# Gates and output projection of a hybrid decoder block as block products of seven multiplications

## The chip, the cores and the metric

The kernel runs on one core of a Trainium2 chip. The metric is the device time of one execution in microseconds (us), and of several runs the median. One execution is also recorded by the profiler, and the rows below come from that one. The engines are named as in the profile: PE is TensorE (matmul), PEld its weight load, DVE is VectorE, ACT is ScalarE, POOL is GpSimd, SP is SyncE. In this kernel SP issues the loads and POOL issues the stores, each as a queue in a fixed order.

## What is computed

One pre-norm decoder block on a sequence of 2048 tokens and 1024 channels (D), in float32, and a last RMS norm. Cut to what matters here:

```python
u = _rmsnorm(h, norm_mix_g[l])
z = jnp.einsum('bsd,dn->bsn', u, w_in[l])
q, k, v, pz, ga, gp = jnp.split(z, offs, axis=-1)
a = _attention_branch(q, k, v).astype(dt)               # (S, 256)
p = _pool_branch(pz, w_pool_grp[l], pool_scale[l]).astype(dt)   # (S, 768)
merged = (jax.nn.sigmoid(ga) * jnp.einsum('bsc,cd->bsd', a, w_att_out[l])
          + jax.nn.sigmoid(gp) * jnp.einsum('bsc,cd->bsd', p, w_pool_out[l]))
h = h + jnp.einsum('bsd,de->bse', merged, w_out[l])
m = _rmsnorm(h, norm_mlp_g[l])
hid = jnp.square(jax.nn.relu(jnp.einsum('bsd,df->bsf', m, w_mlp_in[l])))   # (S, 4096)
h = h + jnp.einsum('bsf,fd->bsd', hid, w_mlp_out[l])
return _rmsnorm(h, norm_final_g)
```

The gates `ga` and `gp` and the output projection `w_out` are products with 1024 x 1024 matrices; the two inner products of `merged` have 256 and 768 input channels.

## The kernel before

Activations lie transposed: 128 channels on the partitions, 512 tokens (a chunk, C) along the row, so a piece is a tile of 128 x 512 and 256 KB. Every operand of a matmul is split in two float32r parts, a rounded high part (a cast on ACT) and the rest (a subtraction on DVE), and each product is made of three matmuls, high x high, high x low and low x high (`mm3` L119, `mm_acc` L612). Such a split costs one ACT and one DVE instruction for each weight and each activation tile.

The stages follow each other on PE: a fold of the pooling weights, then projections and attention (a1, a2, a3, up to L497), then stage b (L506 to L589), the first MLP product c1 (L647 to L744), and the second with the last norm, c2 (L747 to L877). `schedule_with_timeline_sim=True` lets a scheduler put the instructions of each engine in order; each engine then works its list strictly in that order.

At the end of attention (L474 to L497), DVE makes the weights of the three head groups (`nm`), POOL stores them to DRAM (`wts_d`), SP loads them back broadcast over partitions as six tiles `wb` (three buffers), and DVE multiplies and adds these into `af`, which POOL stores to `a_d`.

Stage b goes chunk by chunk, four times: the normed input `u` is computed again from `x` (`norm_x`, L166); for each of 8 output blocks `gate` (L513) loads, splits and multiplies a gate weight; the pooling and the attention product follow, `mf` and `mt` are the gated values, and their sum is split into `mh`, `ml`. Then come 8 blocks of the output projection: the residual `h` is loaded by SP (L575), DVE adds the product from PSUM to it, POOL stores `h` (`h_d`) and the gained `hg` (`hg_d`), ACT squares it and DVE adds the squares up in `hss`, which is stored once per chunk. All products here are plain: 8 x 3 matmuls of 128 x 512 for an output block with 1024 input channels.

Stages c1 and c2 use block products of seven multiplications instead of eight. Weights are taken as 2 x 2 blocks A11 to A22 and activations as 2 x 2 blocks B11 to B22 (halves of the input channels, and the two chunks of one half of the sequence). Sums of weights S1 to S4 and of activations T1 to T4 are made on DVE (`sums` L674), seven products are accumulated in PSUM, and three intermediate results are copied out by ACT (`zS`, `zA`) and added to later products by DVE. In c1 the order of the seven is `ORDER1` (L688), two weight pairs j work side by side, and activations are combined and split once for each half, at its first pairs. PSUM has eight banks. In c2 each half begins with the factor of the MLP norm (`z_st`, a matmul of `hss` with ones, L133, loaded at L798) and the last norm of a chunk (`z_fst`, from `fss`) stands right after its last product (L874, L877).

## Time and profile before

| what | value |
|---|---|
| median of 3 runs | 2897.25 us (2895.51 to 2898.23) |
| the profiled execution | 2892.27 us, its span 2890.5 us |
| mean granted clock of PE | 0.966 |
| PE busy | 2700.0 us, 93%, 13254 matmuls |
| DVE, ACT, POOL busy | 1723.3, 1302.5, 281.9 us |
| DMA | 356.14 MB on the hardware queue (SP), 94.49 MB on the software queue (POOL) |
| first matmul of stage b, first `z_st` of c2 | 829.24, 2193.4 us |

Busy time is summed by engine and says nothing of which stage waits; starts in a row are microseconds from the span's beginning, and `[x <- ...]` behind an instruction is the engine's idle time before it and what ended it.

### The profile page before, as it was taken

To read this page: it belongs to the slowest core of one execution; us is meant where nothing else is said; L and a number is where in the kernel's file an instruction comes from. 1 tells how busy PE (TensorE), PEld (TensorE's weight loads), DVE (VectorE), ACT (ScalarE), POOL (GpSimd) and SP (SyncE) were. 2 spreads that over 40 slices of the span, in tenths; PEclk is the share of its full clock that TensorE was granted. 3 is DMA by queue.
4 is the path that set the end of the run, shared out by engine and by line. 5 is a ranking of instruction groups with operands and counts; after the bars stand their busy time and mean duration, and the time that the engine had idled before them with its cause. 6 is when DMAs were issued, how large, how long until landed. Compare 5 with 4: busy or idle time off the path is not lost.

```text
span 2890.5 us, 36706 instructions
## 1 busy us (share of the span) xinstructions
PE 2700.0 (93%) x13254; PEld 2222.9 (77%) x13254; DVE 1723.3 (60%) x2588; ACT 1302.5 (45%) x2304; POOL 281.9 (10%) x429
## 2 busy tenths in 40 slices
PE   8999999789787999999998999989998999879996
PEld 7887788668676888888886788878886788768885
DVE  5469847455555635446246666766665665757557
ACT  5434444334343424334234555655554444544444
POOL 3034200000000000101000222112221000000000
PEclk9999999899898999999999999999999999989998
DMA  7234443323215544635336555545558556753433
GB/s 259 82 109 165 150 156 112 101 89 111 94 63 182 167 144 134 208 128 187 116 100 207 199 190 189 193 168 181 184 190 312 171 166 196 237 159 108 130 106 128
DMA packets 185030, 452.98 MB, mean 157 GB/s; under 512 B 23216, under 2 KB 30384, under 8 KB 184720
## 3 DMA queue, kind: packets, MB, share of 16 engines
q1 hardware_dynamic: 156096, 356.14, 38.5%
q0 software_dynamic: 28752, 94.49, 8.6%
q8 instruction: 104, 1.70, 0.3%
q14 instruction: 78, 0.64, 0.1%
HBM read 347.68 MB, written 102.86 MB: 156 GB/s over the span
## 4 chain that ended last, share of the span: by engine, by line
PE 46%; issue 41%; DMA 5%; DVE 5%; POOL 2%; ACT 1%; SPq 0%; POOLq 0%; DVEq 0%; ACTq 0%
PE z L616 7%; PE z L617 6%; PE z L615 6%; PE z_b L617 3%; PE z_b L616 3%; PE z_b L615 3%; PE z_c L616 2%; PE z_c L615 2%; PE z_c L617 2%; PE mm_v L270 2%; DMA r<-in_w 1%; PE mm L122 1%; PE mm L124 1%; PE mm L123 1%; DMA x<-hid_d 1%
## 5 line engine op out<-in xcount | busy, mean ns | idle before, releaser
L124 PE MATMUL mmb_bg<-xh_b,lo_bg 128*128 128x512 f32 x512 | 200.1, 391 | 11.6 <-DVE lo_bg L116 11.6
L122 PE MATMUL mmb_bg<-xh_b,hi_bg 128*128 128x512 f32 x512 | 200.0, 391 | 0.0
L123 PE MATMUL mmb_bg<-xl_b,hi_bg 128*128 128x512 f32 x512 | 199.9, 390 | 0.0
L116 DVE TENSOR_TENSOR lo_bg<-raw_bg,hi_bg 128x1024 fp32r<-128x1024 f32 x64 | 78.2, 1222 | 143.2 <-ACT hi_bg L115 143.0
L609 DVE TENSOR_TENSOR wl_S<-r_S,wh_S 128x512 fp32r<-128x512 f32 x128 | 88.4, 690 | 123.7 <-ACT wh_S L608 123.7
L608 ACT CAST wh_S<-r_S 128x512 fp32r<-128x512 f32 x128 | 79.8, 624 | 175.5 <-PE z L616 157.4
L616 PE MATMUL z<-xl_T,wh_S 128*128 128x512 f32 x384 | 149.6, 390 | 2.8 <-DVE xl_T L609 2.8
L617 PE MATMUL z<-xh_T,wl_S 128*128 128x512 f32 x384 | 149.4, 389 | 0.0
L609 DVE TENSOR_TENSOR wl_S<-s,wh_S 128x512 fp32r<-128x512 f32 x128 | 86.6, 689 | 99.8 <-ACT wh_S L608 99.8
L115 ACT CAST hi_bg<-raw_bg 128x1024 fp32r<-128x1024 f32 x64 | 67.4, 1053 | 171.1 <-PE mmb_bg L123 144.3
L615 PE MATMUL z<-xh_T,wh_S 128*128 128x512 f32 x384 | 138.7, 389 | 0.0
L311 ACT ACTIVATE sb_g<-sb_g,negm 128x256 f32<-128x256 f32 (+1 forms) x192 | 86.3, 451 | 96.6 <-DVE negm L309 96.5
L124 PEld LDWEIGHTS mmb_bg<-xh_b,lo_bg 128*128 128x128 f32 x512 | 96.6, 189 | 32.1 <-DVE lo_bg L116 12.0
L609 DVE TENSOR_TENSOR wl_A<-r_A,wh_A 128x512 fp32r<-128x512 f32 x96 | 66.0, 689 | 88.8 <-ACT wh_A L608 88.5
L608 ACT CAST wh_S<-s 128x512 fp32r<-128x512 f32 x128 | 77.2, 618 | 88.6 <-PE z_c L616 43.6
L608 ACT CAST wh_A<-r_A 128x512 fp32r<-128x512 f32 x96 | 59.5, 622 | 123.5 <-PE z L616 88.3
L122 PEld LDWEIGHTS mmb_bg<-xh_b,hi_bg 128*128 128x128 f32 x512 | 96.5, 189 | 20.2
L123 PEld LDWEIGHTS mmb_bg<-xl_b,hi_bg 128*128 128x128 f32 x512 | 96.5, 189 | 20.1
L615 PE MATMUL z<-xh_B,wh_A 128*128 128x512 f32 x256 | 99.4, 404 | 4.6 <-ACT xh_B L608 4.6
L124 PE MATMUL mm_a<-xh_a,lo_a 128*128 128x512 f32 x256 | 102.2, 400 | 0.0
L123 PE MATMUL mm_a<-xl_a,hi_a 128*128 128x512 f32 x256 | 101.7, 398 | 0.0
L616 PE MATMUL z<-xl_B,wh_A 128*128 128x512 f32 x256 | 101.3, 396 | 0.0
(330 smaller groups left out, 8008.5 us busy)
## 6 DMA issues: line engine op xcount, KB each, us to landing
r<-in_w SPq DMA_DIRECT2D x96, 512.0 KB
x<-hid_d SPq DMA_DIRECT2D x160, 256.0 KB
raw_bg<-in_w_gates SPq DMA_DIRECT2D x64, 512.0 KB
r_S<-w2s_d SPq DMA_DIRECT2D x128, 256.0 KB
x_a<-in_xt SPq DMA_DIRECT2D x96, 256.0 KB
r_A<-in_w SPq DMA_DIRECT2D x96, 256.0 KB
raw_a<-in_w_qk SPq DMA_DIRECT2D x32, 512.0 KB
raw_bw<-in_w_o SPq DMA_DIRECT2D x32, 512.0 KB
```

The lines of the kernel that those rows point to most:

```text
L115: nc.scalar.copy(hi, raw)
L116: (lo_on or nc.vector).tensor_sub(lo, raw, hi.bitcast(F32))
L122: nc.tensor.matmul(ps, lh, rh, start=(i == 0), stop=False)
L123: nc.tensor.matmul(ps, lh, rl, start=False, stop=False)
L124: nc.tensor.matmul(ps, ll, rh, start=False, stop=(i == n - 1))
L270: nc.tensor.matmul(pv[t][:, :256], a, b, start=(k == 0 and n == 0), stop=(k == KD - 1 and n == 2))
L311: nc.scalar.activation(s[:, h, :W], s[:, h, :W], AF.Exp, bias=negm[:, col + h:col + h + 1], accum_out=l[:, col + h:col + h + 1])
L608: nc.scalar.copy(hi, src)
L609: nc.vector.tensor_sub(lo, src, hi.bitcast(F32))
L615: nc.tensor.matmul(ps, lh, rh, start=start and i == 0, stop=False, skip_group_check=True)
L616: nc.tensor.matmul(ps, lh, rl, start=False, stop=False, skip_group_check=True)
L617: nc.tensor.matmul(ps, ll, rh, start=False, stop=stop and i == n - 1, skip_group_check=True)
```

## The change

Stage b is taken out. `norm_x`, as attention calls it, now also stores `u` to DRAM (`u_d`), with three buffers instead of two. One pool `wp` serves four kinds of stages, each run for half of the sequence (1024 tokens): `gates` (the 16 gate blocks as block products of `u_d`, sigmoid on ACT, stored to `sg_d`), `merge` (the pooling and attention products as before, with the gates loaded back, stored to `mg_d`), `residual` (the output projection as block products of `mg_d`) and `mlp_in` (c1 as before). In `residual` the block leaves PSUM as the intermediate tiles do; a DMA of POOL with `accum_op` adds `xt` into the tile, another stores it to `h_d`, ACT squares it, a third DMA adds the squares up in DRAM (`hss_d`), ACT multiplies by the gain in place, and a fourth stores to `hg_d`. The order of the stages is written at the end: gates of half 0, merge 0, gates 1, residual 0, merge 1, mlp_in 0, residual 1, mlp_in 1. In c2 the factor is made at the second of the seven products, and the last norms are put off to the seventh weight pair of the product that comes next.

```diff
+    u_d = dram.tile([KD, P, SEQ], F32, name="u_d")
+    sg_d = dram.tile([2 * KD, P, SEQ], F32, name="sg_d")
+    mg_d = dram.tile([KD, P, SEQ], F32, name="mg_d")
...
-        u = io.tile([P, C], F32, name=f"u_{key}", tag="xu", bufs=2)
+        u = io.tile([P, C], F32, name=f"u_{key}", tag="xu", bufs=3)
...
-            normed(load_x(c, k, key), g_mix[:, k:k + 1], rstd[:, c * C:(c + 1) * C], hi, lo, f"{key}_{k}")
+            u = normed(load_x(c, k, key), g_mix[:, k:k + 1], rstd[:, c * C:(c + 1) * C], hi, lo, f"{key}_{k}")
+            nc.gpsimd.dma_start(u_d[k, :, c * C:(c + 1) * C], u)
...
-    with ExitStack() as st:
-        bp = pool_of(st, "b")
...
-            ssq = bp.tile([P, C], F32, name=f"hss_{c}", tag="hss", bufs=1)
-            for e in range(KD):
-                w = split_load(w_o[e], D, f"bw_{c}_{e}")
-                h = bp.tile([P, C], F32, name=f"h_{c}_{e}", tag="h", bufs=3)
-                nc.sync.dma_start(h, xt[c, :, e, :])
-                ps = ps_b(f"bw_{c}_{e}")
-                mm3_chunk(ps, w, (mh, ml))
-                nc.vector.tensor_add(h, ps, h)
-                nc.gpsimd.dma_start(h_d[e, :, c * C:(c + 1) * C], h)
-                hg = bp.tile([P, C], F32, name=f"hg_{c}_{e}", tag="hg", bufs=2)
-                nc.scalar.mul(hg, h, g_mlp[:, e:e + 1])
-                nc.gpsimd.dma_start(hg_d[e, :, c * C:(c + 1) * C], hg)
-                if e == 0:
-                    nc.scalar.square(ssq, h)
-                else:
-                    sq = bp.tile([P, C], F32, name=f"hsq_{c}_{e}", tag="hsq", bufs=2)
-                    nc.scalar.square(sq, h)
-                    nc.vector.tensor_add(ssq, ssq, sq)
-            nc.gpsimd.dma_start(hss_d[c], ssq)
...
+    RAWB, SB, WB, ZB = 4, 5, 5, 12
...
+    def stage(key, weights, n_pairs, make, fin, extra=None):
+        m = {}
+        for j0 in range(0, n_pairs, 2):
+            js = (j0, j0 + 1)
+            w, bank, mid = {}, {}, {}
+            for j in js:
+                a11, a12, a21, a22 = raws((weights[2 * j], weights[2 * j + 1]), f"{key}_{j}")
+                s1, s2, s3, s4 = sums(a11, a12, a21, a22, f"{key}_{j}")
+                w[j] = {"A11": a11, "A12": a12, "A22": a22, "S1": s1, "S2": s2, "S3": s3, "S4": s4}
+            for n, step in enumerate(ORDER1):
+                a, b, bk = step.split()
+                if j0 == 0:
+                    m[b] = make(b)
+                for j in js:
+                    kj = f"{key}_{j}"
+                    wh, wl = split(wp, w[j][a], f"{kj}_{a}", "w", WB)
+                    first = (j, bk) not in bank
+                    if first:
+                        bank[j, bk] = ps_c(f"{kj}_{bk}")
+                    ps = bank[j, bk]
+                    mm_acc(ps, [(wh[:, k * P:(k + 1) * P], wl[:, k * P:(k + 1) * P], *m[b][k])
+                                for k in range(KH)], first, True)
+                    if n in (0, 1, 2):
+                        t = mid[j, n] = wtile(f"z{a}_{kj}")
+                        nc.scalar.copy(t, ps)
+                    elif n < 6:
+                        t = mid[j, {3: 2, 4: 1, 5: 0}[n]]
+                        nc.vector.tensor_add(t, ps, t)
+                        fin(j, *{3: (0, 1), 4: (1, 1), 5: (0, 0)}[n], t, None)
+                    else:
+                        fin(j, 1, 0, wtile(f"zc_{kj}"), ps)
+            if extra:
+                extra(j0 // 2)
...
+    def gates(hf):
+        def fin(j, row, t, z, ps):
+            nc.scalar.activation(z, z if ps is None else ps, AF.Sigmoid)
+            nc.gpsimd.dma_start(sg_d[2 * j + row, :, at(hf, t)], z)
+        stage(f"g{hf}", w_gates, KD, inputs(u_d, hf, f"g{hf}"), fin)
...
+                sp, sa = wtile(f"sp_{key}", "h22", KH), wtile(f"sa_{key}", "tt", KH)
+                nc.sync.dma_start(sp, sg_d[KD + e, :, at(hf, t)])
+                nc.sync.dma_start(sa, sg_d[e, :, at(hf, t)])
+                pp, pq = ps_c(f"pp_{key}"), ps_c(f"pq_{key}")
+                mm_acc(pp, [(w[k // 3][0][:, k % 3 * P:(k % 3 + 1) * P], w[k // 3][1][:, k % 3 * P:(k % 3 + 1) * P],
+                             *pa[t, k]) for k in range(6)], True, True)
+                o = e % 2 * 2 * P
+                mm_acc(pq, [(wa[0][:, o + k * P:o + (k + 1) * P], wa[1][:, o + k * P:o + (k + 1) * P],
+                             *pa[t, 6 + k]) for k in range(2)], True, True)
+                nc.vector.tensor_mul(sp, pp, sp)
+                nc.vector.tensor_mul(sa, pq, sa)
+                z = wtile(f"mg_{key}")
+                nc.vector.tensor_add(z, sp, sa)
+                nc.gpsimd.dma_start(mg_d[e, :, at(hf, t)], z)
...
+    def residual(hf):
+        def fin(j, row, t, z, ps):
+            e, c = 2 * j + row, 2 * hf + t
+            if ps is not None:
+                nc.scalar.copy(z, ps)
+            nc.gpsimd.dma_start(z, xt[c, :, e, :], accum_op=ALU.add)
+            nc.gpsimd.dma_start(h_d[e, :, at(hf, t)], z)
+            sq = wtile(f"sq_{c}_{e}")
+            nc.scalar.square(sq, z)
+            nc.gpsimd.dma_start(hss_d[c], sq, **({"accum_op": ALU.add} if (j, row) != FIRST else {}))
+            nc.scalar.mul(z, z, g_mlp[:, e:e + 1])
+            nc.gpsimd.dma_start(hg_d[e, :, at(hf, t)], z)
+        FIRST = (0, 0)
+        stage(f"o{hf}", w_o, KD // 2, inputs(mg_d, hf, f"o{hf}"), fin)
...
+    gates(0)
+    merge(0)
+    gates(1)
+    residual(0)
+    merge(1)
+    mlp_in(0)
+    residual(1)
+    mlp_in(1)
...
+                if n == 1:
+                    r2s = [factor(hf, t) for t in range(2)]
...
+                    if j == 6 and due:
+                        norm(*due.pop())
...
-                    norm(hf, 1, y1, ssqs[1])
+                    due.append((hf, 1, y1, ssqs[1]))
...
-                    norm(hf, 0, y0, ssqs[0])
+                    due.append((hf, 0, y0, ssqs[0]))
```

The listed matmul rows of PE go from 12004 to 11727. Two places follow where the order of an engine changes: the end of attention, on SP and on DVE, and the output projection, on POOL.

SP's queue at the end of attention, before: `wb` are the six broadcast loads of the last chunk, `raw_bg` and `raw_bp` weights of stage b, `h` the residual loads.

```order
L112 DMA raw_bg_0_7_7510<-in_w_gates 128x1024
L112 DMA raw_bp_0_7580<-in_w_pool 128x768
L490 DMA wb_0_0_7196<-wts_d 128x1x512
L490 DMA wb_0_1_7199<-wts_d 128x1x512
L490 DMA wb_1_0_7202<-wts_d 128x1x512
L490 DMA wb_1_1_7206<-wts_d 128x1x512
L490 DMA wb_2_0_7210<-wts_d 128x1x512
L112 DMA raw_bp_1_7609<-in_w_pool 128x768
L490 DMA wb_2_1_7214<-wts_d 128x1x512
L112 DMA raw_bp_2_7638<-in_w_pool 128x768
```

The same place after: `r_g` are the first gate weights, `hx_g` and `h_g` the first pieces of `u_d`.

```order
L495 DMA wb_1_1_7241<-wts_d 128x1x512
L495 DMA wb_2_0_7245<-wts_d 128x1x512
L495 DMA wb_2_1_7249<-wts_d 128x1x512
L607 DMA r_g_0_0_7267<-in_w_gates 128x1024
L607 DMA r_g_0_1_7269<-in_w_gates 128x1024
L607 DMA r_g_1_0_7279<-in_w_gates 128x1024
L607 DMA r_g_1_1_7281<-in_w_gates 128x1024
L559 DMA hx_g_B_0_0_7291<-u_d 128x512
L559 DMA hx_g_B_1_0_7297<-u_d 128x512
L559 DMA hx_g_B_2_0_7303<-u_d 128x512
```

All gate weights of the first chunk (`raw_bg_0_0` to `raw_bg_0_7`) stood ahead of the last `wb` loads; the first load of the new stage stands behind the sixth.

DVE at the same place, after: `af` gathers the broadcast weights, `wl_g` is the low part of a gate weight, `s_g` its sums, `mB11l` the low part of an activation.

```order
L501 TENSOR_TENSOR af_7230<-af_7230,wb_2_0_7245 128x512
L500 TENSOR_TENSOR wb_2_1_7249<-wb_2_1_7249,o2c_7228 128x512
L501 TENSOR_TENSOR af_7230<-af_7230,wb_2_1_7249 128x512
L528 TENSOR_TENSOR wl_g_0_A_7316<-r_g_0_0_7267,wh_g_0_A_7315 128x512
L597 TENSOR_TENSOR s_g_0_7271<-r_g_0_1_7269 128x512
L598 TENSOR_TENSOR s_g_0_7272<-s_g_0_7271,r_g_0_0_7267 128x512
L599 TENSOR_TENSOR s_g_0_7274<-r_g_0_0_7267,s_g_0_7272 128x512
L600 TENSOR_TENSOR s_g_0_7273<-r_g_0_0_7267,r_g_0_1_7269 128x512
L528 TENSOR_TENSOR wl_g_1_A_7335<-r_g_1_0_7279,wh_g_1_A_7334 128x512
L528 TENSOR_TENSOR wl_g_0_S_7394<-s_g_0_7271,wh_g_0_S_7393 128x512
L597 TENSOR_TENSOR s_g_1_7283<-r_g_1_1_7281 128x512
L528 TENSOR_TENSOR mB11l_g_0_7294<-hx_g_B_0_0_7291,mB11h_g_0_7293 128x512
```

The first low part stands behind the last `af`; before, the low parts of all eight gate weights of the first chunk stood ahead of it.

POOL's queue in the output projection before, at the start of a chunk: one store of `h` and one of `hg` for each block.

```order
L579 DMA h_d<-h_0_10832 128x512
L579 DMA h_d<-h_1_10871 128x512
L582 DMA hg_d<-hg_0_10861 128x512
L582 DMA hg_d<-hg_1_10900 128x512
L579 DMA h_d<-h_2_10912 128x512
L579 DMA h_d<-h_3_10953 128x512
L582 DMA hg_d<-hg_2_10941 128x512
L582 DMA hg_d<-hg_3_10982 128x512
L579 DMA h_d<-h_4_10994 128x512
```

POOL's queue in `residual` of half 0 after, second two weight pairs (`zS`, `zA` are the tiles of the intermediate results, L699 the accumulating DMA into the tile, L700 the store of `h`, L703 the accumulating DMA into `hss_d`, L705 the store of `hg`).

```order
L699 DMA zS_o_2_11331<-in_xt 128x512
L699 DMA zS_o_3_11349<-in_xt 128x512
L700 DMA h_d<-zS_o_2_11331 128x512
L703 DMA hss_d<-sq_4_11370 128x512
L699 DMA zS_o_2_11294<-in_xt 128x512
L700 DMA h_d<-zS_o_3_11349 128x512
L699 DMA zS_o_3_11313<-in_xt 128x512
L703 DMA hss_d<-sq_6_11394 128x512
L705 DMA hg_d<-zS_o_2_11331 128x512
L699 DMA zA_o_2_11256<-in_xt 128x512
L700 DMA h_d<-zS_o_2_11294 128x512
L699 DMA zA_o_3_11275<-in_xt 128x512
```

Two DMAs of a block have become four, and each `h_d` store stands behind the accumulating DMA into the same tile, with one or two other issues between.

## Rows read from the trace of the kernel before

**Rows 1.** Page, busy us (share) xinstructions; then the chain that ended last.
```profile
PE 2700.0 (93%) x13254; PEld 2222.9 (77%) x13254; DVE 1723.3 (60%) x2588; ACT 1302.5 (45%) x2304; POOL 281.9 (10%) x429
...
PE 46%; issue 41%; DMA 5%; DVE 5%; POOL 2%; ACT 1%; SPq 0%; POOLq 0%; DVEq 0%; ACTq 0%
```

**Rows 2.** Chain of waits, two chunks of stage b: start, us, what.
```profile
1027.10 142.23 issue
1201.18 142.23 issue
```

**Rows 3.** Stretches: us; PE, PEld, DVE, ACT, POOL busy; clock, DMA share, GB/s.
```profile
1027.00:1201.00 174.00, 174.00 (x769) 144.09 (x768) 84.06 (x105) 65.37 (x90) 9.13 (x18) 1.00 0.49 159
1550.00:1610.00 60.00, 47.58 (x180) 34.70 (x180) 50.34 (x82) 35.48 (x64) 7.48 (x14) 0.92 0.63 199
2195.00:2205.00 10.00, 1.54 (x3) 0.84 (x3) 7.23 (x13) 9.13 (x13) 0.54 (x1) 0.64 1.00 366
2520.00:2530.00 10.00, 1.60 (x8) 0.98 (x6) 9.45 (x17) 2.37 (x4) 0.00 (x0) 0.78 0.92 312
2530.00:2540.00 10.00, 3.99 (x4) 1.00 (x4) 4.03 (x6) 4.07 (x5) 0.00 (x0) 0.50 0.44 128
2540.00:2550.00 10.00, 0.84 (x2) 0.50 (x2) 8.75 (x14) 5.59 (x7) 0.00 (x0) 0.50 0.44 156
```

**Rows 4.** PE in order of time, stage b's first matmul and longest gap.
```profile
829.24 0.50 PE L122 MATMUL mmb_bg<-xh_b,hi_bg 128*128 128x512 f32 x1
879.68 0.79 PE L124 MATMUL mmb_bg<-xh_b,lo_bg 128*128 128x512 f32 x1 [11.61 <-DVE lo_bg L116]
```

**Rows 5.** Matmuls of one tile: ns shortest/mean/longest, first to last start.
```profile
L133 PE MATMUL z_st<-hss,ones x8: 590/1059/1221, 2193.4 to 2550.3; 128*128 128x512 f32 x8
```

**Rows 6.** PE in order of time, c1: start, us, operation, [idle before it].
```profile
1550.98 1.22 PE L615 MATMUL z_b<-mB11h,wh_A 128*128 128x512 f32 x2 [5.26 <-ACT mB11h L608]
1602.67 0.39 PE L615 MATMUL z_b<-mB11h,wh_A 128*128 128x512 f32 x1
1888.26 0.80 PE L615 MATMUL z_b<-mB11h,wh_A 128*128 128x512 f32 x1 [7.67 <-ACT wh_A L608]
```

**Rows 7.** TensorE in the last stage (c2), its gaps.
```profile
2203.46 2.07 PE L133 MATMUL z_st<-hss,ones 128*128 128x512 f32 x2 [9.05 <-DMA hss<-hss_d]
2535.00 2.07 PE L133 MATMUL z_fst<-fss,ones 128*128 128x512 f32 x2 [13.40 <-DVE fss L777]
```

**Rows 8.** VectorE at the end of attention, in order of time.
```profile
842.64 1.73 DVE L480 TENSOR_TENSOR nm<-nm,mn 4x1536 f32<-4x1536 f32 x1
855.02 0.69 DVE L493 TENSOR_TENSOR af<-wb,ot 128x512 f32<-128x512 f32 x1 [9.52 <-DMA wb<-wts_d]
883.90 0.69 DVE L496 TENSOR_TENSOR af<-af,wb 128x512 f32<-128x512 f32 x1
```

**Rows 9.** SyncE's queue at the end of attention.
```profile
847.37 14.67 SPq L490 DMA_DIRECT2D wb<-wts_d  x5
872.64 0.50 SPq L490 DMA_DIRECT2D wb<-wts_d  x1
```

**Rows 10.** Groups by line: busy us, mean ns of one, then idle before.
```profile
L609 DVE TENSOR_TENSOR wl_S<-s,wh_S 128x512 fp32r<-128x512 f32 x128 | 86.6, 689 | 99.8 <-ACT wh_S L608 99.8
L731 POOL DMA_DIRECT2D hid_d<-zS x64 | 34.7, 542 | 89.7 <-ACT zS L719 72.9 <-DVE zS L740 16.1 <-issue 0.6
```

**Rows 11.** Instructions of two tiles of the output projection, columns as before.
```profile
L581 ACT ACTIVATE hg<-h,colt x32: 708/724/731, 996.0 to 1546.5; 128x512 f32<-128x512 f32 x32
L587 ACT ACTIVATE hsq<-h x28: 612/617/634, 997.7 to 1547.2; 128x512 f32<-128x512 f32 x28
```

**Rows 12.** DMA by tile: queue, count, KB each, median us from issue to landing.
```profile
h_d<-h POOLq DMA_DIRECT2D x32, 256.0 KB, 4.2
hid_d<-zS POOLq DMA_DIRECT2D x64, 256.0 KB, 5.3
p_d<-pf POOLq DMA_DIRECT2D x24, 256.0 KB, 2.4
```

More of the change, by code (lines that the diff above doesn't have):

```diff
@@ L660, in make @@
-                out.append(split(cp, src, f"{hf}_{kk}", "m" + name, KH))
-            return out
-        def w2_sums(j):
-            raw = []
-            for f in (2 * j, 2 * j + 1):
-                r = cp.tile([P, D], F32, name=f"r2_{f}", tag="raw", bufs=RAWB)
-                nc.sync.dma_start(r, w_2[f])
-                raw.append(r)
-            a11, a21, a12, a22 = (r[:, i * C:(i + 1) * C] for r in raw for i in range(2))
-            for i, s in enumerate(sums(a11, a12, a21, a22, f"2_{j}")):
-                nc.gpsimd.dma_start(w2s_d[i][j], s)
@@ new lines, in make, with sums @@
+                    x = t1s[kk]
+                    nc.vector.tensor_sub(x, b21s[kk], x)
+                out.append(split(wp, x, f"{key}_{kk}", "m" + name, KH))
+            return out
+        return make
+    def sums(a11, a12, a21, a22, key):
+        s1, s2, s3, s4 = (wtile(f"s{i}_{key}", "s", SB) for i in range(1, 5))
+        nc.vector.tensor_add(s1, a21, a22)
+        nc.vector.tensor_sub(s2, s1, a11)
+        nc.vector.tensor_sub(s4, a12, s2)
+        nc.vector.tensor_sub(s3, a11, a21)
+        return s1, s2, s3, s4
@@ new lines, in mlp_in, with put, fin, w2_sums @@
+    def mlp_in(hf):
+        blocks = {}
+        def put(i, j, t):
+            nc.gpsimd.dma_start(hid_d[hf][i][j], t)
+        def fin(j, row, t, z, ps):
+            nc.scalar.activation(z, z if ps is None else ps, AF.Relu)
+            nc.scalar.square(z, z)
+            if (row, t) == (0, 1):
+                blocks[j] = z
+            elif (row, t) == (1, 1):
+                put(2, j, z)
+                d = wtile(f"zd_{hf}_{j}")
+                nc.vector.tensor_sub(d, z, blocks[j])
+                put(4, j, d)
+            elif (row, t) == (0, 0):
+                put(0, j, z)
+                b12 = blocks.pop(j)
+                nc.vector.tensor_sub(b12, b12, z)
+                put(3, j, b12)
+            else:
+                put(1, j, z)
+        def w2_sums(n):
+            j = hf * (NPR // 2) + n
+            a11, a21, a12, a22 = raws((w_2[2 * j], w_2[2 * j + 1]), f"w2_{j}")
+            for i, s in enumerate(sums(a11, a12, a21, a22, f"w2_{j}")):
+                nc.gpsimd.dma_start(w2s_d[i][j], s)
+        stage(f"c{hf}", w_1, NPR, inputs(hg_d, hf, f"c{hf}"), fin, w2_sums)
```

218 lines of the change are left out of this document (65 added, 153 removed).

## The prediction

> **What bounds the kernel now.** The page comes first. PE is busy for 2700.0 of 2890.5 us, and the chain that ended last is 46% PE and 41% "issue" [rows 1]: for most of the span the time is set by the number of matmuls, so a change that takes matmuls away gains, unless it opens gaps. The two things to read are therefore the price of a matmul and the gaps of each stage.
>
> The price: the chain has two equal pieces of stage b, one chunk each, that start 174.08 us apart [rows 2]; a chunk has 768 matmuls of 128x512 (384 gates, 192 merge, 192 output projection), and the window over the same stretch counts 769 [rows 3]. So one costs 174.08/768 = 0.2267 us at a granted clock of 1.00. The mean listed durations are longer because matmuls overlap.
>
> The gaps: stage b starts at 829.24 [rows 4], and c2's first matmul at 2193.4 [rows 5]. The 1364.2 us between hold 3072 matmuls of stage b and 2688 of c1, 5760 x 0.2267 = 1305.8. Only 58.4 us are lost there. In stage b the largest gap is 11.61 us [rows 4]: its first weights were split early. c1 loses more: its first weight pair, 168 matmuls or 38.1 us, takes from 1550.98 to 1602.67, 51.7 us, and at its second half PE waits 7.67 us [rows 6]. The reason is visible in the window from 1550: DVE is busy 50.34 of 60 us [rows 3]. A first pair wants 72 DVE instructions (28 low parts of activations, 16 activation sums, 14 low parts of weights, 8 weight sums, 6 additions to intermediates), 72 x 0.689 [rows 10] = 49.6 us. So each start of a seven-multiplication stage is bound by DVE by up to 49.6 - 38.1 = 11.5 us, unless its work is done ahead. c2 loses about 27 us between its halves: in three windows from 2520 to 2550 there are 14 matmuls, 3.2 us worth [rows 3].
>
> **The change part by part.** I sum against the profiled execution, 2892.27 us, and add 4.98 at the end, by which the median 2897.25 lies above it.
>
> *Matmuls.* Gates go from 1536 to 1344 and the output projection from 768 to 672 (seven eighths); merge and c1 stay. 288 x 0.2267 = -65.3 us. The listed PE rows fall by 277, which agrees. All 5472 that remain cost 1240.5.
>
> *Start of the gates, half 0.* Before, the loads and splits of the first eight gate weights stood ahead of the broadcast loads `wb` that end attention, so PE ran while these trickled in. Now the first gate loads stand behind the sixth `wb` on SP, and DVE's first low part behind the last `af`. In the trace the weights `nm` are ready at 842.64 + 1.73, the first `wb` is used at 855.02 and the last `af` at 883.90 [rows 8]; SP issues the last `wb` only at 872.64 [rows 9], as there are three buffers. PE has nothing of the new stage until then. From 884.6 the first pair takes about the 49.6 us of DVE, and the last 24 matmuls (5.4) trail: 939.6, where an unhindered PE would be at 829.2 + 38.1 = 867.3. Loss 72; I take 71, as some casts are early. If the weights' store and the `wb` loads took 2.4 us each, as `p_d` in a quiet stretch [rows 12], the 12 `af` operations of 0.69 would end at 844.4 + 4.8 + 8.3 = 857.5, a loss of 45; if the second pair also stands cold, as after c1's first, 76.
>
> *Other starts.* There are six more: merge 0, gates 1, residual 0, mlp_in 0, residual 1, mlp_in 1 (merge 1's work stands among the residual's, below). Bounds are 0 (all made ahead) and 11.5 each, 69 together. c1's second start was not made ahead before and cost its gap of 7.67 us and, as I estimate, 3 more for matmuls behind it at a lower clock (after c2's first gap the granted clock is 0.64, a mixture of the levels of 1.2 and 2.4 GHz [rows 3]): about 11. I take 11 for residual 0, residual 1 and mlp_in 1, 7 for gates 1 and mlp_in 0, which follow a merge that leaves DVE time, 4 for merge 0: 51.
>
> *Residual.* Each block now passes accumulate (A from issue to landing), then the store of `h` (D), and in ACT square and gain (0.62 + 0.72 [rows 11]), the last in place and so only after D. POOL works its list in order, and two blocks of a pair go side by side: a weight pair's eight blocks take 4 x (A + D + 1.34). The cover is its matmuls, 38.1 us. Issuing is not the limit: 32 DMAs x 0.542 [rows 10] = 17.3. No accumulating DMA is in the trace. The nearest rows are plain stores of the same 256 KB: 2.4 in a quiet stretch, 4.2 for `h`, 5.3 for `hid_d` [rows 12]. With 2.4 for both the chain is 25 us and hidden; with 4.2 it is 39; with 5.3, 47.8. The upper bound is an accumulate that costs twice the store: A = 8.4, D = 4.2 gives 55.8, and 10.6 with 5.3 gives 69. ACT's copies of the next pair stand behind the squares and gains, so the excess over 38.1 reaches PE, less the three blocks of 12 matmuls, 8.2 us, that PE can run ahead in its eight banks. I take A = 6, D = 4.5, between the busy rows and twice them, since the stage moves much: weights 4.2, activations 6.3, `xt` 4.2, `h` 4.2, squares 4.2, `hg` 4.2 MB, together 27 MB in 76 us or 358 GB/s, near the 366 of the fullest window [rows 3]. Excess 47.4 - 38.1 = 9.3 per pair, 18.6 per half, less 8.2: 10.4, twice 21. Bounds: 0, and 2 x (2 x 30.9 - 8.2) = 107.
>
> The nearest rule speaks for less: the Trainium skill, "DMA: Bandwidth & Descriptors", section "Anatomy of one DMA — SWDGE (gpsimd) path", fits a DMA of this queue as 2.0 us plus its bytes over 436 GB/s, 2.6 us for 256 KB. The quiet row agrees (2.4), the busy rows are twice that (4.2 and 5.3), so I don't use it; by the page's fit the chain would be hidden and the sum 21 us lower.
>
> *Stores of `u`.* 32 issues of POOL, 17 us, lie under attention, where PE is the bound; three buffers that wait for a landing each could delay a chunk's start by a few us. I take 0, at most 12.
>
> *c2.* The factor moved to the second product takes away the 9.05 us gap at the start [rows 7], but DMA is fully used there (share 1.00 [rows 3]), so I take 6 of it. Between the halves the 13.40 us wait for `fss` [rows 7] goes, and the waits for `hss` behind it, as the next product's matmuls stand ahead; a cold operand remains: 22 of 27. Together -28; bounds -9 and -36.
>
> *Sum.* Losses after: 71 + 51 + 21 = 143, before 58.4: +84.6. With -65.3 and -28: -8.7. So 2883.6, and on the median's basis about 2889 us. The gain in matmuls is paid back by starts and by the residual's chain.
>
> **The rivals.**
>
> *Accumulate costs twice.* Place: POOL's chain in the two residual stages. Reading a destination as well makes A about 8.4 to 10.6. It decides from the point where A + D passes 9.5 - 1.34 = 8.2 us, plus 1 for the free banks. With 8.4 and 4.2 the loss is 2 x (2 x 17.7 - 8.2) = 54, with 10.6 and 5.3 it is 107, against 21. By bytes: 16 more reads of 262 KB twice over are 8.4 MB per half, 23 us at 366 GB/s, so 46 for both. I take +45: 2934, between 2918 and 2955. For it: the stage is near the fullest rate already, and three busy stores landed at 4.2 to 5.3. Against it: the DMA share over a chunk of stage b is 0.49 [rows 3], so engines are free outside bursts.
> The Trainium skill states such a rule: "Collectives: The Full Stack", section "The bandwidth ceiling: the fold count and why AG ≠ RS ≠ AR", says that an add in the DMA engine is slow for its two source reads, about half the rate. No run here shows it yet; it is this rival's mechanism.
>
> *The new stages are fed in time.* Stores land in 2.4 to 4.2 us, the chain is hidden (-21), and the scheduler has laid enough splits ahead that the six starts cost half (-25); if the `wb` loads come faster, less still. 2889 - 21 - 25 = 2843 at the best; half of that gain, 2866, is the value I give. For it: DVE is 60% busy overall, and merge uses it little. Against it: c1's own second start was not covered.
>
> *No change on PE*: that the matmuls don't fall is excluded by the listed rows.
>
> **How the numbers follow.** A measurement here tells about 0.2% from no change, so faster means below 2891.5 and slower above 2903. My forecast has 0.40, with its own range 2872 to 2908; the slow rival 0.32, the fast one 0.28. Of the forecast's 0.40 I put 0.20 below 2891.5, 0.13 within and 0.07 above. Faster 0.28 + 0.20 = 0.48, same 0.13, slower 0.39. The range that leaves out the outer ends of both rivals is 2850 to 2938.
>
> **What would show it.** PE should be about 65 us less at full rate; the windows from 829 to 885 should hold nearly no matmuls, and DVE should release PE until about 940. At the two residual stages I look for ACT's copies waiting on the accumulate, and for the landing of L699 and L700: A of 6 and D of 4.5 bear out the term, A above 8 the slow rival, both under 4 the fast one. Between c2's halves the gaps should be under 8 us in all. The prediction is wrong if PE's idle time at the start of the gates is under 40 us, or if the residual stages lose over 50.

## The result, and the profile after

The changed kernel takes 2914.71 us (median of 4 runs, 2913.35 to 2918.79) against 2896.38 for the kernel before on the same chip: 1.0069 times, 95% interval 1.0051 to 1.0086. It is slower: inside the stated range, but above the kernel before, where the forecast of 2889 lay below it. Its profiled execution took 2918.79 us. The runs below are compared by their ratios to the kernel before on the same chip; each ratio is known to some 0.15%, so a difference between two of them to about 6 us.

The page after, busy time by engine and then the chain by engine, beside [rows 1]:

```profile
PE 2652.3 (91%) x12966; PEld 2177.2 (75%) x12966; DVE 1815.4 (62%) x2848; ACT 1355.0 (46%) x2504; POOL 405.8 (14%) x617
...
PE 47%; issue 35%; DMA 9%; DVE 4%; POOL 3%; ACT 1%; SPq 0%; POOLq 0%; DVEq 0%; ACTq 0%
```

PE has 288 matmuls less, and is 48 us less busy in a span that is 26 longer. On the chain, DMA has gone from 5% to 9%: PE waits for something that waits for landings. PE's waits show where, by line and what ended them (us in total, times, longest):

```profile
PE z_g_b L534 <- ACT mB11h_g L527: 60.3, 1, 60.3
...
PE z_o_b L534 <- ACT zA_o L637: 26.1, 2, 13.7
PE z_c_b L534 <- ACT zA_c L637: 21.5, 1, 21.5
...
PE z_fst L136 <- DVE fss L784: 9.0, 1, 9.0
```

The first is the start of the gates. The second is the second weight pair of each residual stage, the third the stage behind the last residual; both wait for ACT's copy of an intermediate tile. `z_fst`, which cost 13.40 us between the halves of c2 [rows 7], now appears only at the end; between the halves the waits come to 1.1 us.

A stage's loss is its length, from its first matmul to the next stage's first, less its matmuls at 0.2267 us. Matmuls that run slower behind a wait are in the loss too: after 1372.42 they start 0.43 us apart, at a granted clock of 0.55 from 1372 to 1378. PE's list in order of time gives these starts in the changed kernel: attention's last group of matmuls 829.0, gates 890.3, merge 1054.3, gates 1141.3, residual 1305.5, merge 1402.1, mlp_in 1504.0, residual 1816.3, mlp_in 1924.0, c2 2255.2. The columns to the right are for three of the runs below.

| loss, us | forecast | changed | act_free | spx_hss | wbpe_spx_hss |
|---|---|---|---|---|---|
| gates 0, with the idle time before it | 71 | 73.0 | 74.0 | 73.6 | 49.8 |
| merge 0 | 4 | -0.1 | 1.3 | 0.5 | 0.7 |
| gates 1 | 7 | 11.9 | 12.0 | 10.4 | 11.1 |
| residual 0 | 21.4 | 20.4 | 4.2 | 5.9 | 5.7 |
| merge 1 | 0 | 14.8 | 16.4 | 6.6 | 6.2 |
| mlp_in 0 | 7 | 7.6 | 7.3 | 10.8 | 11.8 |
| residual 1 | 21.4 | 31.5 | 15.0 | 17.5 | 16.3 |
| mlp_in 1 | 11 | 26.5 | 14.3 | 14.5 | 14.4 |
| sum | 143 | 185.6 | 144.5 | 139.8 | 116.0 |

c2 takes 2916.7 - 2255.2 = 661.5 us, before 2890.5 - 2193.4 = 697.1 [rows 5]: 35.6 less. The account closes: -65.3 for matmuls, +127.2 for losses (185.6 - 58.4), -35.6 in c2 make +26.3, and the spans differ by 26.2.

### The profile page after: what moved, and what is told of

The parts are those of the page before. It is cut to its first block, busy times and chain, and to the rows that moved or that the text cites. A ratio compares the mean times of both kernels' runs of the same rounds, so it can differ in the third digit from the quotient of the medians.

```text
span 2916.7 us, 37152 instructions
## 1 busy us (share of the span) xinstructions
PE 2652.3 (91%) x12966; PEld 2177.2 (75%) x12966; DVE 1815.4 (62%) x2848; ACT 1355.0 (46%) x2504; POOL 405.8 (14%) x617
## 4 chain that ended last, share of the span: by engine, by line
PE 47%; issue 35%; DMA 9%; DVE 4%; POOL 3%; ACT 1%; SPq 0%; POOLq 0%; DVEq 0%; ACTq 0%
PE z L535 6%; PE z L536 6%; PE z L534 6%; PE z_c_b L534 3%; PE z_c_b L536 3%; PE z_c_b L535 3%; PE z_c_c L534 2%; PE z_c_c L536 2%; PE z_c_c L535 2%; PE mm_v L275 2%; DMA x<-hid_d 1%; POOL sg_d L654 1%; PE mm L125 1%; PE mm L126 1%; PE mm L127 1%
## 5 line engine op out<-in xcount | busy, mean ns | idle before, releaser
L528 DVE TENSOR_TENSOR wl_c_S<-s_c,wh_c_S 128x512 fp32r<-128x512 f32 x128 | 86.8, 688 | 94.7 <-ACT wh_c_S L527 94.5
L527 ACT CAST wh_c_S<-s_c 128x512 fp32r<-128x512 f32 x128 | 77.2, 616 | 75.9 <-PE z_c_c L535 41.0
L321 PE MATMUL t_g<-ident,sb_g 128*128 128x128 f32 x300 | 67.0, 315 | 43.9 <-ACT sb_g L316 43.4
L125 PE MATMUL mm_a<-xh_a,hi_a 128*128 128x512 f32 x256 | 99.8, 398 | 1.4 <-ACT qk L410 1.4
L536 PE MATMUL z<-xh_B,wl_A 128*128 128x512 f32 x256 | 98.2, 392 | 0.0
L527 ACT CAST wh_c_A<-r_c 128x512 fp32r<-128x512 f32 x96 | 59.5, 620 | 69.2 <-PE z_c_b L535 27.1
L535 PEld LDWEIGHTS z<-xl_T,wh_S 128*128 128x128 f32 x384 | 72.1, 188 | 18.6 <-DVE xl_T L528 3.7
L528 DVE TENSOR_TENSOR wl_c_A<-r_c,wh_c_A 128x512 fp32r<-128x512 f32 x96 | 65.8, 685 | 29.7 <-ACT wh_c_A L527 29.7
L534 PEld LDWEIGHTS z<-xh_T,wh_S 128*128 128x128 f32 x384 | 72.1, 188 | 15.1
```

What stands on the lines that cost most here:

```text
L125: nc.tensor.matmul(ps, lh, rh, start=(i == 0), stop=False)
L321: nc.tensor.transpose(ps_t[:, b, h * P:(h + 1) * P], s[:, h, b * P:(b + 1) * P], ident)
L527: nc.scalar.copy(hi, src)
L528: nc.vector.tensor_sub(lo, src, hi.bitcast(F32))
L534: nc.tensor.matmul(ps, lh, rh, start=start and i == 0, stop=False, skip_group_check=True)
L535: nc.tensor.matmul(ps, lh, rl, start=False, stop=False, skip_group_check=True)
```

## The residual stages: what holds PE

DMA of the changed kernel by tile, as in [rows 12] (count, KB, median us to landing); `zS_o<-in_xt` is the accumulate of L699, `h_d<-zS_o` the store of L700; half of the blocks leave from `zS`, the others from `zA` and `zc`:

```profile
hss_d<-sq POOLq DMA_DIRECT2D x32, 256.0 KB, 6.5
...
zS_o<-in_xt POOLq DMA_DIRECT2D x16, 256.0 KB, 7.1
h_d<-zS_o POOLq DMA_DIRECT2D x16, 256.0 KB, 6.3
hg_d<-zS_o POOLq DMA_DIRECT2D x16, 256.0 KB, 7.1
...
zA_o<-in_xt POOLq DMA_DIRECT2D x8, 256.0 KB, 7.7
...
zc_o<-in_xt POOLq DMA_DIRECT2D x8, 256.0 KB, 6.1
```

Over all 32 blocks the medians are 7.1 for the accumulate and 5.8 for the store; I had taken 6 and 4.5. ACT's list between the first and second pair of residual 0, in order of time, with idle time and its end in brackets:

```profile
1359.67 0.57 ACT L698 COPY zc_o<-z_o_b 128x512 f32<-128x512 f32 x1
...
1365.73 0.63 ACT L702 ACTIVATE sq<-zc_o 128x512 f32<-128x512 f32 x1 [0.57 <-DMA zc_o<-in_xt]
1366.27 0.57 ACT L698 COPY zc_o<-z_o_b 128x512 f32<-128x512 f32 x1
1366.73 0.62 ACT L527 CAST wh_o_S<-s_o 128x512 fp32r<-128x512 f32 x1
1368.95 0.72 ACT L704 ACTIVATE zc_o<-zc_o,colt 128x512 f32<-128x512 f32 x1 [1.60 <-DMA h_d<-zc_o]
1371.26 0.63 ACT L702 ACTIVATE sq<-zc_o 128x512 f32<-128x512 f32 x1 [1.59 <-DMA zc_o<-in_xt]
1371.80 1.05 ACT L637 COPY zA_o<-z_o_b 128x512 f32<-128x512 f32 x2
```

ACT waits for the h store (D), then for the accumulate (A), and only then copies the next pair's zA; PE's next matmul starts at 1372.42. Two explanations fit. In the first, ACT's in-order list carries the landings to PE. In the second the DMA engines are full and everything is late. The stretches are the two residual stages and the start of mlp_in 1, with PE's wait of 21.5 us; the columns are as in [rows 3]:

```profile
1305.50:1402.00 96.50, 81.09 (x333) 65.55 (x332) 46.90 (x75) 44.39 (x80) 33.19 (x47) 0.89 0.79 209
...
1816.30:1924.00 107.70, 82.34 (x334) 66.10 (x335) 56.82 (x91) 46.82 (x84) 34.57 (x52) 0.87 0.77 206
1924.00:1962.00 38.00, 16.46 (x63) 13.05 (x62) 24.32 (x40) 24.98 (x44) 16.89 (x25) 0.69 0.98 248
```

Only the last of them has a share near 1. In the residual stages it is 0.79 and 0.77 in the mean, not the 0.90 that two of the expectations below name, and at most 0.95 in the windows read (1850 to 1890).

### acc_plain: the add left out

```diff
-            nc.gpsimd.dma_start(z, xt[c, :, e, :], accum_op=ALU.add)
+            nc.gpsimd.dma_start(z, xt[c, :, e, :])
```

> The changed kernel with the residual's DMA a plain load instead of an accumulating one (the product of the output projection is overwritten, so the output is not the block's). Same issues, same waits. Theory 'the add in the DMA is dear' (two reads): A falls from about 7.0 to 5 us or less, the rounds of the chain get 2 us shorter, 16 rounds, so 25 to 35 us faster. Rival 'the traffic makes every landing slow': A stays within 1 us of 7 and the time within 12 us of the changed kernel's 2914.7.

2901.09 us, ratio 1.0027 (1.0016 to 1.0038), 0.42% below the changed kernel's ratio, about 12 us. Landing of the same DMAs:

```profile
zS_o<-in_xt POOLq DMA_DIRECT2D x16, 256.0 KB, 5.5
...
zA_o<-in_xt POOLq DMA_DIRECT2D x8, 256.0 KB, 6.1
zc_o<-in_xt POOLq DMA_DIRECT2D x8, 256.0 KB, 6.0
```

7.1 against 5.5 and 7.7 against 6.1: for these tiles an accumulating DMA takes 1.3 times as long as a plain one to land, for `zc` no longer (6.1 against 6.0), over all 32 blocks 1.2 times (7.1 against 5.8), and nowhere twice. The gain is below the 25 that the first theory asked and at the edge of the rival's 12. Residual 0, merge 1, residual 1 and mlp_in 1 together lose 72.8 us in this trace, in the changed kernel 93.2. So the add is a part of the loss, but not the whole.

### early and hg_own: one wait out of the list

```diff
+                        if pre:                    # early: behind the first copy
+                            pre(j, *{2: (0, 1), 1: (1, 1), 0: (0, 0)}[n], t)
```
```diff
-            nc.scalar.mul(z, z, g_mlp[:, e:e + 1])
+            g = wtile(f"hg_{c}_{e}")               # hg_own
+            nc.scalar.mul(g, z, g_mlp[:, e:e + 1])
```

> The changed kernel with the accumulating DMA of the residual issued right behind ACT's first copy out of PSUM, while the second product of the block is still to come; only the blocks with one product (zc) keep it at the end. Same DMAs, same bytes. Theory 'chain of landings' (A then D in POOL's order): A leaves the chain for three of four blocks, rounds of about D + 1.3 = 7 us, 28 per pair against 38 of matmuls: some 40 to 60 us faster than 2914.7. Rival 'bytes' (DMA share 0.90 in these stages): within 10 us of 2914.7.

> The changed kernel with the gained block written to a tile of its own, so that ACT's multiplication no longer waits for the landing of the h store (D) from the same tile. Same DMAs, same bytes, accumulating as in the change. Theory 'chain of landings in order': a round of two blocks falls from A + D + 1.3 = 14 us to A + 1.3 = 8.4 us, four rounds 34 us against 38 of matmuls; the residual's losses fall by 25 to 45 us. Rival 'bytes, DMA engines full at 0.9': under 10 us faster than 2914.7.

early: 2900.80 us, 1.0021 (1.0011 to 1.0030), about 14 us, between the two. hg_own: 2935.76 us, 1.0151 (1.0125 to 1.0176), 24 us slower, against both. In the traces 12 of the 24 us stand in these four stages, and 7 already in attention, which the edit does not touch. ACT's list of hg_own at the same place:

```profile
1369.27 0.57 ACT L698 COPY zc_o<-z_o_b 128x512 f32<-128x512 f32 x1
...
1378.28 0.63 ACT L702 ACTIVATE sq<-zc_o 128x512 f32<-128x512 f32 x1 [6.37 <-DMA zc_o<-in_xt]
1378.82 0.70 ACT L705 ACTIVATE hg<-zc_o,colt 128x512 f32<-128x512 f32 x1
1379.43 0.56 ACT L698 COPY zc_o<-z_o_b 128x512 f32<-128x512 f32 x1
1387.07 0.63 ACT L702 ACTIVATE sq<-zc_o 128x512 f32<-128x512 f32 x1 [7.08 <-DMA zc_o<-in_xt]
1387.61 0.70 ACT L705 ACTIVATE hg<-zc_o,colt 128x512 f32<-128x512 f32 x1
1388.22 1.05 ACT L637 COPY zA_o<-z_o_b 128x512 f32<-128x512 f32 x2
```

Here, as in the changed kernel, the copy of the pair's second zc stands behind the square of the first, so the second accumulate is issued only after the first has landed. From the first zc's copy to zA's it takes 19.0 us, in the changed kernel 12.1. The two landings took 7.4 and 5.8 us from their issue, in the changed kernel 5.1 and 4.1, and ACT's casts were done before, so that it stood idle for 6.37 + 7.08. Why these landings are longer is not shown. early left these two accumulates where they were, as zc has one product only. My sum of A + D for each round is not borne out as a formula: hg_own takes D out of ACT's list and is slower. What counts is which landings stand in ACT's list ahead of the next copy.

### cp_o and cp_oc: copies on DVE

```diff
-                        nc.scalar.copy(t, ps)
+                        (nc.vector.tensor_copy if key[0] == "o" else nc.scalar.copy)(t, ps)
```

> The changed kernel with the copies of a block's first product out of PSUM made by DVE in place of ACT, in the two residual stages only. All accumulating DMAs stay as they are, the same bytes move. Theory 'ACT's list': PE waits at the second pair because ACT's copies stand behind squares that wait for the accumulate's landing; then the two waits of PE for zA of 12.4 and 13.7 us go and the time is 20 to 35 us below 2914.7. Rival 'bytes, full DMA engines': the waits move to another instruction and the time stays within 8 us.

> As the run before it, and the copies of the first pair of the second mlp_in by DVE too. Theory 'ACT's list': the 21.5 us wait of PE at the start of that stage (for ACT's copy of zA behind the last residual squares) goes as well, 10 to 20 us below the run before it. Rival 'operands late': at that place the next operands, which come from the hg stores, are as late, and it gains under 5 us.

2914.22 us, 1.0067 (1.0052 to 1.0082), and with the first pair of mlp_in 1 as well 2913.18, 1.0065 (1.0050 to 1.0080): no change. By the time alone the rival wins. DVE's list in cp_o tells otherwise:

```profile
1369.01 0.69 DVE L528 TENSOR_TENSOR wl_o_S<-s_o,wh_o_S 128x512 fp32r<-128x512 f32 x1 [5.26 <-ACT wh_o_S L527]
1369.62 1.28 DVE L637 COPY zA_o<-z_o_b 128x512 f32<-128x512 f32 x2
```

DVE's copy stands behind a low part that waits for a weight cast, and that cast stands in ACT's list behind the same squares. PE's two waits for zA_o are still 8.1 and 12.4 us, now for DVE. In the residual stages the wait changed engine, not its source. For the start of mlp_in 1 see act_free.

### act_free: nothing on ACT waits for a landing

The square and the gained block are made before the residual is added, so `hss_d` and `hg_d` lack the residual; all DMAs stay. ACT still waits for loads, and for tiles that a store frees.

```diff
+            nc.scalar.square(sq, z)
+            nc.scalar.mul(g, z, g_mlp[:, e:e + 1])
             nc.gpsimd.dma_start(z, xt[c, :, e, :], accum_op=ALU.add)
             nc.gpsimd.dma_start(h_d[e, :, at(hf, t)], z)
-            nc.scalar.square(sq, z)
-            nc.scalar.mul(z, z, g_mlp[:, e:e + 1])
```

> The changed kernel with the square and the gained block made from the product before the residual is added (so the residual is missing in the squares and in hg), the gained block in a tile of its own. The same DMAs with the same bytes, but no ACT instruction waits for the landing of an accumulate or of the h store. Theory 'ACT's list': PE's waits for zA and for weight casts at the second pair and at the next stage go; the losses from the first residual to c1 fall from 101 us by 40 or more, 2875 or less. Rival 'bytes, full DMA engines': loads land late and the stores free their tiles late all the same; within 15 us of 2914.7.

2880.61 us, ratio 0.9958 (0.9942 to 0.9975): 1.1% below the changed kernel, some 32 us, with the gained block in the same extra tile that cost hg_own 24 us. It misses the expected 2875 by 6, and is far outside the rival's 15. The landings got slower, PE's waits shorter:

```profile
zS_o<-in_xt POOLq DMA_DIRECT2D x16, 256.0 KB, 7.9
h_d<-zS_o POOLq DMA_DIRECT2D x16, 256.0 KB, 7.4
```
```profile
1868.22 0.80 PE L534 MATMUL z_o_b<-mT2h_o,wh_o_S 128*128 128x512 f32 x1 [3.25 <-ACT zA_o L637]
1916.86 0.80 PE L534 MATMUL z_c_b<-mT2h_c,wh_c_S 128*128 128x512 f32 x1 [6.57 <-ACT zA_c L637]
```

3.25 for 13.69 and 6.57 for 21.54. That decides it for the residual stages: they lose 4.2 and 15.0 us instead of 20.4 and 31.5, with the same bytes, so there the landings reach PE through ACT's list.

At the start of mlp_in 1 it decides less, as the edit also makes the gained block earlier, and with it the `hg` stores and the loads from `hg_d`. In the changed kernel these operands are as late as the copy:

```profile
1951.65 0.62 ACT L527 CAST mB22h_c<-h_c_T 128x512 fp32r<-128x512 f32 x1 [0.72 <-DMA h_c_T<-hg_d]
...
1953.93 0.62 ACT L527 CAST mT2h_c<-tt_c 128x512 fp32r<-128x512 f32 x1 [0.52 <-DVE tt_c L580]
...
1956.03 1.05 ACT L637 COPY zA_c<-z_c_b 128x512 f32<-128x512 f32 x2
```

The product behind the copy wants four pieces of T2, and the last is cast at 1953.93. In cp_oc, with this copy on DVE, PE waits as long, since DVE too works on these operands first:

```profile
1949.17 0.77 PE L534 MATMUL z_c_b<-mT2h_c,wh_c_S 128*128 128x512 f32 x1 [23.70 <-DVE zA_c L637]
```

So cp_oc's rival, late operands, stands there beside ACT's list, and no run separates the two.

Merge 1 still loses 16.4 us in act_free, and there the second explanation has its place: PE waits for casts, and these for loads, at a DMA share of 1.09 from 1390 to 1420.

```profile
1412.47 0.62 ACT L527 CAST mT4h_pa<-pa 128x512 fp32r<-128x512 f32 x1 [3.83 <-DMA pa<-p_d]
```

Merge 1 loses as much in spx below (16.2), without accumulates into the tile, and 6.6 in spx_hss, without those into `hss_d` as well.

### spx and spx_hss: no accumulating DMA

```diff
+        def pre(j, row, t, z, ps):                 # in place of ACT's copy
+            nc.sync.dma_start(z, xt[2 * hf + t, :, 2 * j + row, :])
+            nc.vector.tensor_add(z, ps, z)
...
-            nc.gpsimd.dma_start(z, xt[c, :, e, :], accum_op=ALU.add)
...
-            nc.gpsimd.dma_start(hss_d[c], sq, **({"accum_op": ALU.add} if (j, row) != FIRST else {}))
+                nc.vector.tensor_add(ssq[t], ssq[t], sq)          # spx_hss only
```

> The changed kernel with the residual's input loaded by SP and added by DVE while it copies the block's first product out of PSUM, in place of ACT's copy and the accumulating DMA; the sum of squares is still accumulated by DMA. Theory 'chain of landings': rounds of D + 1.3 us, hidden by the matmuls, 45 to 65 us faster than 2914.7. Rival 'bytes': the same 16 x 256 KB move on another queue, without a second read, under 20 us faster. Rival 'DVE': 32 more DVE operations of 0.69 us, 11 per stage, in a stage where DVE is about 45 of 59 us busy: gains half of what it saves.

> The changed kernel without any accumulating DMA: the residual's input comes by SP and is added by DVE as it copies the first product out (as in the run with the accumulating DMA into the tile taken out), and the squares are summed by DVE in two tiles, stored once per chunk. To make room there are 11 instead of 12 tiles for results. Against that run (2889): theory 'accumulating into DRAM loads the DMA engines and POOL's order' says 15 to 25 us faster, as 32 transfers of 256 KB that read twice and their waits go; rival 'DVE is the bound in these stages' says no gain or slower, as 28 additions of 0.69 us come to DVE.

spx: 2889.18 us, 0.9988 (0.9976 to 1.0000), about 23 us below the changed kernel, half of what the first theory expected, as the rival 'DVE' had it; whether for its reason is not shown. Of PE's 26.1 us of waits for zA_o 2.1 are left, and the residual stages lose 6.4 and 15.1 us. spx_hss: 2877.24, 0.9940 (0.9921 to 0.9959), another 14 us, just under the 15 to 25 expected. It comes in merge 1 and in mlp_in 1, which lose 16.2 and 21.3 in spx. So the squares' accumulates cost about as much as the add into the tile; their landings were no item of my sum.

### o_plain: output projection plain again

```diff
-        stage(f"o{hf}", w_o, KD // 2, inputs(mg_d, hf, f"o{hf}"), fin)
+                nc.sync.dma_start(z, xt[c, :, e, :])
...
+                nc.vector.tensor_add(z, ps, z)
+                nc.gpsimd.dma_start(h_d[e, :, at(hf, t)], z)
```

> The changed kernel with the output projection as plain products again (768 matmuls instead of 672, 21.8 us more), in the same place in the order of stages; the residual's input comes by SP, DVE adds it out of PSUM, the squares are still accumulated in DRAM by DMA. Theory 'the residual's chain of landings costs more than its eighth of matmuls saves': the stages from the first residual to c1 lose 95 us in the changed kernel; without chain and with fewer DVE operations about 30, so 65 - 22 = about 40 us faster than 2914.7. Rival 'the stores to DRAM and the accumulated squares make the loss, in whatever form': within 15 us of 2914.7.

2883.61 us, 0.9960 (0.9945 to 0.9975): 32 us faster than the changed kernel with 96 matmuls more. Its residual stages lose 2.6 and 0.0 us; merge 1 and mlp_in 1 still lose 16.4 and 21.0. The block form of this stage, as the change made it, costs more than its eighth of the matmuls. Most of the 32 us comes from the accumulate into the tile, which o_plain drops too: spx, in block form without it, is already 23 us faster, and o_plain another 8.

## The start of the gates, and c2

In the changed kernel the first four broadcast loads come to use 5.3 to 5.4 us apart, at a DMA share of 0.12 from 845 to 865: it is not full engines that delay them. PE's first matmul of the gates after, and in wbpe, where six small matmuls with a selector replace the store and the six broadcast loads of the last chunk:

```profile
890.32 1.22 PE L534 MATMUL z_g_b<-mB11h_g,wh_g_A 128*128 128x512 f32 x2 [60.25 <-ACT mB11h_g L527]
```
```profile
842.54 2.04 PE L500 MATMUL wbp<-nm,sel 4*128 4x512 f32 x2 [14.19 <-DVE nm L490]
...
862.73 1.22 PE L544 MATMUL z_g_b<-mB11h_g,wh_g_A 128*128 128x512 f32 x2 [3.88 <-ACT mB11h_g L537]
```
```diff
-                nc.sync.dma_start(wb, src)
+                if c == NCH - 1:
+                    wp_ = psum.tile([P, 2, C], F32, name=f"wbp_{g}_{hp}", tag="s")[:, 0, :]
+                    nc.tensor.matmul(wp_, sel[:, hp, :], nm[:, g, :], start=True, stop=True)
```

> The changed kernel with one thing else: the weights of the last attention chunk are spread over the partitions by six float32 matmuls with a selector (PE is idle there) instead of a store to DRAM and six broadcast loads. Theory 'the six loads hold SP and DVE and so the start of the gates' : DVE ends the last af near 858 instead of 885, the gates' first matmul comes near 860 instead of 890, the time is 25 to 30 us below 2914.7. Rival 'the first loads of u and of the gate weights are late anyway' : under 10 us.

2896.09 us, 1.0011 (1.0001 to 1.0020): about 17 us, the start 28 us earlier. The rest went into later stages: gates 0 and mlp_in 0 lose 2 and 5 us more.

> The kernel before with the edits of c2 and the last chunk's weights spread by PE. Theory 'the six loads cost only where the stage behind them can't start early': stage b's own gap there was 11.6 us, so 2866.1 falls by 0 to 10 us, not by the 20 that it brought to the changed kernel. Rival 'the loads cost the same in both': about 20 us faster, 2846, and then the block products of gates and output projection bring nothing beside the best version.

The same edit on the kernel before with c2's edits: 2879.49 us, 0.9958 (0.9944 to 0.9972), against 0.9901 without it: 16 us slower, against both theories. There PE has gate matmuls to do, from 828.6 on in b_c2, and in its in-order list the selector matmuls hold them up until 856.6:

```profile
840.31 2.04 PE L495 MATMUL wbp<-nm,sel 4*128 4x512 f32 x2 [14.19 <-DVE nm L485]
```

The first output projection then starts 8 us later, and the spans of the two traces differ by 7.6; the rest of the 16 is not in them. In the changed kernel PE was idle there only because of the change.

> The kernel before with only the edits of c2 (factor at the second product, last norms put off to the seventh weight pair of the next product). In the changed kernel c2 took 2916.7 - 2255.2 = 661.5 us, before 2890.5 - 2193.4 = 697.1, so 35.6 less. Theory 'c2 gains by itself': about 35 us faster than before, 2861 on the median. Rival 'c2 gained because the stage ahead of it left DMA or operands in better order': under 20 us, as c2's start before was at full DMA use.

b_c2 (the kernel before with the edits of c2 alone, as in the diff of the change): 2866.09 us, 0.9901 (0.9886 to 0.9915), 29 us faster where 35 were expected. So this part of the change is right; the rest costs about 1.7%, some 49 us.

## The versions that come of it

> Both together: no accumulating DMA, and the last chunk's weights spread by PE. If the two losses are apart in time and add up, the gain is the sum of the two runs' gains: 2889 - 20 - 28 = about 2841, below the kernel before by 1.9%. If the wait moves to a later stage, 2860 to 2870.

spx_hss and wbpe together: 2851.40 us (2850.93 to 2852.33), 0.9850 (0.9835 to 0.9865). That is between the 2841 of gains that add up and the 2860 of a wait that moves. It beats the kernel before by 1.5% and b_c2 by 0.5%. Against spx_hss the selector brings 26 us, against the changed kernel 17; the difference of 9 is about as large as its uncertainty.

> The version without accumulating DMAs and with the weights spread by PE (2851.4), and the gained block in a tile of its own as well. Losses of the stages from the first residual to c1 are 54 us there; if D still holds ACT's copies, 10 to 20 us faster; if what is left is the start of each stage (DVE), under 5; if the ring of 11 tiles gets short, slower.

> The same version (2851.4) with the 16 activation sums of each gates stage done by POOL in place of DVE. Theory 'the first pair of a stage is bound by DVE' (72 operations, 49.6 us against 38.1): the two gates stages start 8 to 11 us quicker each, about 16 to 20 us faster. Rival 'POOL slows DVE or is late itself' (a POOL subtraction of 128x1024 took 2.55 us): no gain, or slower.

> The version without accumulating DMAs and with the last weights spread by PE (2851.4), with the copies of the first pair of the second mlp_in by DVE. There PE waits 7.0 us for ACT's zA copy at that place. Theory 'ACT's list': about 5 us faster. Rival 'DVE is the bound of a first pair': no gain, or up to 5 us slower.

> The version without accumulating DMAs and with the last weights spread by PE (2851.4), with the output projection as plain products (96 matmuls, 21.8 us more). There the two residual stages lose 22 us in block form, and the merge and the MLP stage behind them 20. Theory 'block form of the output projection is worth its eighth once nothing accumulates by DMA': 5 to 15 us slower, about 2861. Rival 'the stage is bound by DVE in block form': within 4 us of 2851, or faster.

Four edits on it, and none is faster. The gained block in its own tile: 2854.70, 0.9875 (0.9859 to 0.9891). Activation sums of the gates on POOL: 2858.56, 0.9890 (0.9871 to 0.9908). Copies of the first pair of mlp_in 1 on DVE: 2851.49, 0.9849 (0.9832 to 0.9865). Output projection plain, squares on DVE: 2858.88, 0.9877 (0.9861 to 0.9893). The first comes out slower, as was said for a ring of tiles that gets short, the third as its rival said; neither cause was traced.

By the time, 8 us, the block form of the output projection would be worth some of its 21.8 once nothing accumulates by DMA. By the stages it isn't: from the first residual to c2 the block form loses 54.5 us and the plain one 32.7, 21.8 less, which is the price of the 96 matmuls. The two traces differ by 6.2 us, and 4.6 of these stand in c2, which the edit does not touch. So a gain by the block form is not shown.

The POOL version lost in its first gates stage, which loses 24.3 us instead of 14.4 behind its first matmul; a sum there took 1.3 to 1.8 us in the mean of its group, and PE waited for B21 and its splits:

```profile
L601 POOL TENSOR_TENSOR tt_g<-hx_g_B,tt_g 128x512 f32<-128x512 f32 x4 | 7.2, 1818 | 4.4 <-DMA hx_g_B<-u_d 4.4
```

That a first pair is bound by DVE is therefore neither shown nor refuted by it: the sums came late instead.

## Why the prediction was wrong

*Matmuls* and the *price of a matmul*: right; the account closes with -65.3.

*Start of the gates*: 71 forecast, 73.0 measured, by the way described (890.3 for the first matmul, DVE busy 46.14 of the 52 us behind it).

*Other starts*: gates 1 11.9 for 7, mlp_in 0 7.6 for 7, merge 0 nothing for 4: 19.4 for 18 in sum. The other three, 33 in the forecast, lose 4.2, 15.0 and 14.3 in act_free, where no square and no gain waits for the add or for the store of `h`: 33.5, though not 11 each.

*c2*: 35.6 for 28, of which b_c2 shows 29 by itself; this hid some 8 us of what follows.

*Residual*: this step failed. It was priced at 21, with starts of 33 beside it, 54 for residual 0, merge 1, residual 1 and mlp_in 1; these lost 93.2. The two residual stages alone lost 51.9, just over the 50 that the prediction had set as its sign of being wrong. The mechanism, ACT's copies behind squares and gains that wait for landings, was right in the residual stages: in act_free they lose 19.2. The size was wrong in three ways.

First, the landings: 7.1 and 5.8 in the median of all blocks instead of 6 and 4.5. I had taken values beside the busy rows of 4.2 and 5.3 for a stage that I had myself put at 358 GB/s. It moved 209 and 206 GB/s at shares of 0.79 and 0.77, and the landings were longer all the same. With the measured values the step's sum is 4 x (7.1 + 5.8 + 1.34) = 57.0 a pair, so 2 x (2 x 18.9 - 8.2) = 59, and 92 with the starts, where 93.2 were lost. That it comes so near is in part luck: the rounds do not follow each other as the sum has them (hg_own), and the two points below were not in it.

Second, the place: I charged the last pair's excess inside the stage, but of the 39 us above the forecast 30 stand in merge 1 and mlp_in 1. In mlp_in 1 no run separates ACT's copies from late operands out of `hg_d`.

Third, merge 1, which I had put at nothing, as its work stood among the residual's. It lost 14.8, and 16.4 in act_free. The accumulates of the squares, whose landings had no price in the sum, make most of it: with them it loses 16.2 in spx, without them 6.6 in spx_hss.

On the profiled executions, in which the sum was made, I was too fast by 35 us (-8.7 for +26.3); on the medians by 26.

*The rivals*: the slow one, 2934, had the right side and its place in part, and too strong a cause. The add makes a landing 1.2 to 1.3 times as long, not twice; leaving it out brought 12 us by the time, 20 in the four stages of the trace, of the 39 that I was short there. The rule of half the rate for two source reads (the Trainium skill, "Collectives: The Full Stack", section "The bandwidth ceiling: the fold count and why AG ≠ RS ≠ AR"), which the page gives for the reduce step of a collective, is not borne out for a landing here. Nor is the fit of 2.6 us (the Trainium skill, "DMA: Bandwidth & Descriptors", section "Anatomy of one DMA — SWDGE (gpsimd) path") in these stages, where plain stores of `h` landed at 5.8. The fast rival fails: the landings are longer than the 4.2 us that it allowed, and the starts cost what was forecast.
